# Half chunks of a run-ahead stage spread over the groups beside them, and a residual made in sixteen pieces beside another projection

## The chip, the cores and the metric

One core of a Trainium2 chip runs the whole kernel. The metric is device time in microseconds of one execution; three runs of the kernel before gave 2915.17, 2918.57 and 2919.74 us, median 2918.57 us. TensorE is called PE here, VectorE DVE, ScalarE ACT, GpSimd POOL and SyncE SP.

## What is computed

One decoder layer over 16 meta tokens and 1,024 positions of width 1,024, in float32. The reference, cut to what matters here:

```python
h = layer_norm(concat([meta, x]), ln_emb_g, ln_emb_b)
q, k, v, xr, gr = split(h @ w_in)                      # 5 x 512 columns
attn = stick_breaking(q, k, v)                         # 8 heads
lru = rg_lru(causal_conv(xr)) * gelu(gr)               # gated linear recurrence
mixed = concat([rms_norm(attn), rms_norm(lru)]) @ w_out
h = layer_norm(ALPHA * h + mixed, ln1_g, ln1_b)
# PEER: 8 heads pick 16 of 128 x 128 experts for every token
s1, s2 = q1 @ keys1, q2 @ keys2; idx, g = top_k of the sums, softmax
act = gelu(down[idx] . h); ffn = sum(g * act * up[idx])
h = layer_norm(ALPHA * h + ffn, ln2_g, ln2_b); return h[16:]
```

## The kernel before

The tokens lie in tiles of 128. The program has these stages.

**Front.** Nine tiles `xt` of x are loaded and normalised in place (line 281), transposed and split into a high and a low float32r part `hT`. Each product is three matmuls (`mm3`, lines 127 to 129). While the tiles come, the first two columns of the recurrence's input are projected (`convs`). Then the residual ALPHA * (g * xt + b) is made on DVE from the tiles where they lie (lines 306 and 307, two operations of 128x1024 for each of 8 tiles) and stored by SP to `xh_d` (line 308). The buffers of `xt` are freed with that. Next come the convolution (line 354), the value projection (`values`, in two halves of 256 columns, with its weights split into `v` on ACT and DVE by lines 123 and 124), the gates (line 366, from weights that POOL clears at line 361), the recurrence and the gate branch. Attention follows. In its last quarter `lru_load` reads the residual back (line 561).

**Queries.** Scores and top-16 for six of the eight token tiles. Between them `run_ahead` does chunks of the dense part.

**The dense part.** For the first five tiles (640 tokens) every expert is computed. The experts are 128 chunks of 128. A chunk's down product is two halves of 24 matmuls of 128x320 into the PSUM tile `dps` (`down_gelu`, line 854), each half evicted with a gelu by ACT (line 861). A chunk that is run ahead takes a prepared weight (`take`, line 838: one load in flight, one weight split by ACT and DVE ahead) and its result goes to DRAM, `ge_d`, and comes back later as `gex` (line 1124). 56 chunks are run ahead before: 2 in the output mix, 23 among the queries, 31 in the gate-matrix stage, by the table `RAG = (6, 7, 6, 6, 6)`.

**Gate-matrix stage** (lines 1005 to 1037). For each of five tiles `j` there are 16 groups of 8 tokens. A group compares on DVE (`bt`, `ae`, lines 1020 and 1025), scales on ACT (`at_`, line 1027, eight times), multiplies on PE (`g`, line 1030, 8 products, which the profile shows as 16 matmuls), evicts on ACT into `gst` (line 1031), does one gathered row of a sparse tile on DVE (`hyb`) and a step of the top-16 of the last two tiles (`topk_turn`). Every fourth group SP writes `gst`, 2 MB, to `Gd` (line 1035). After the 16 groups of a tile the written order has that tile's run-ahead chunks:

```python
            for c in range(RAG[j]):
                run_ahead()
```

**Main stage.** For the remaining chunks the down product is made, multiplied with the gate matrix read back from `Gd` as `gl` (line 1117), split into `wh` and `wl`, and multiplied with the `up` rows into `ups` and `keep` (line 1161 on). The sparse rows of the last two tiles (`row`, line 898) are gathered beside it in proportion to PE's work (`tick`).

A scheduler orders each engine's instructions when the program is built: it follows the written order as a priority and its own estimate of times, except where an instruction is pinned. Each engine then runs its list in order, and each DMA queue too.

Of the kernel before, what the change touches and what calls it, by code (L numbers as in the profile page):

```python
# [8 lines left out]
F32 = mybir.dt.float32  # L9
# [5 lines left out]
ALU = mybir.AluOpType  # L15
# [54 lines left out]
RAG = (6, 7, 6, 6, 6)  # L70
RAM = {7: 2}
RA = sum(RAM.values()) + sum(RAQ.values()) + sum(RAG)
# [4 lines left out]
def layer_kernel(ctx, tc, x, meta, vecs, chan, lnc, w_in, gate_w, w_out, wq, skT, down, downT, up, out, dbg=None):  # L77
# [10 lines left out]
    xh_d = dram.tile([S, D], F32, name="xh_d")  # L88
    al_d = dram.tile([KC, P, S], F32, name="al_d")
# [99 lines left out]
    with ExitStack() as c1:  # L189
# [53 lines left out]
        with ExitStack() as c2:  # L243
# [34 lines left out]
            for j0, j1 in LNB:  # L278
                for j in range(j0, j1):
                    n = NM if j == 0 else P  # L280
                    A.activation(xts[j][:n], xts[j][:n], AF.Identity, bias=nm9[:n, j:j + 1], scale=rs9[:n, j:j + 1])
                c0 = 0 if j0 == 0 else NM + (j0 - 1) * P
# [18 lines left out]
            eg = load_vec(ga, 0, "eg")  # L301
            eb = load_vec(ga, 1, "eb")
            A.activation(eg, eg, AF.Copy, scale=ALPHA)
            A.activation(eb, eb, AF.Copy, scale=ALPHA)
            for j in range(1, NT + 1):
                V.tensor_tensor(xts[j], xts[j], eg, op=ALU.mult)
                V.tensor_tensor(xts[j], xts[j], eb, op=ALU.add)
                SY.dma_start(xh_d[(j - 1) * P:j * P, :], xts[j])

        with ExitStack() as c2:  # L310
            vt = ap.tile([P, NB, AW], F32, name="vt")

            with ExitStack() as c3:
# [3 lines left out]
                mps = c3.enter_context(tc.tile_pool(name="mps", bufs=1, space=PSUM, reuse_waits="tile"))  # L317
                sp8 = lr.tile([P, 4], F32, name="sp8")
# [26 lines left out]
                ts_ = [lr.tile([P, T], F32, name=f"t_{i}") for i in range(4)]  # L345

# [32 lines left out]
                def values(half, vh):  # L379
                    for b in range(NB):  # L380
                        t0 = 0 if b == 0 else NM + (b - 1) * P
                        ps = pps.tile([P, 512], F32, name="pp")
                        for c in range(KC):
                            mm3(ps[:, :256], hT[0][:, c, t0:t0 + P], hT[1][:, c, t0:t0 + P], vh[0][:, c], vh[1][:, c], c == 0, c == KC - 1)
                        m = NM if b == 0 else P
                        A.activation(vt[:m, b, half * 256:half * 256 + 256], ps[:m, :256], AF.Copy)

# [15 lines left out]
                for i in range(4):  # L403
                    sq = l2.tile([P, T], F32, name="ig")
                    V.tensor_tensor(sq, rs_[i], rs_[i], op=ALU.mult)
                    V.scalar_tensor_tensor(ts_[i], sq, 1.0, ts_[i], op0=ALU.add, op1=ALU.mult)
                    A.activation(ts_[i], ts_[i], AF.Sqrt)
                    V.tensor_tensor(ys[i], ys[i], ts_[i], op=ALU.mult)
                    V.tensor_tensor_scan(ts_[i], rs_[i], ys[i], 0.0, op0=ALU.mult, op1=ALU.add)
                ms = mps.tile([P, NT], F32, name="ms")  # L410
# [147 lines left out]
            def lru_load(j):  # L558
                mh, ml = mixed(4, j)
                hr = wr.tile([P, D], F32, name="raw")  # L560
                SY.dma_start(hr, xh_d[j * P:(j + 1) * P, :])
# [292 lines left out]
    def down_gelu(c, dps, ge, tick=None):  # L854
        hi, lo = ddn.pop(c)
        for i in range(2):
# [5 lines left out]
            if tick:  # L862
                tick(KC * 3 * HN)

    ra = iter(range(RA))

    def run_ahead():
        c = next(ra)
        ddn[RAS[c]] = take()
        ge = geps[0].tile([P, NF], F32, name="ge")  # L870
        down_gelu(RAS[c], dps1, ge)
        SY.dma_start(ge_d[c], ge)
# [73 lines left out]
    with ExitStack() as c1:  # L946
# [55 lines left out]

        iob = gc.tile([P, NKEYS, AEW], BF16, name="iob")
        G.iota(iob, pattern=[[1, NKEYS], [0, AEW]], base=0, channel_multiplier=0, allow_small_or_imprecise_dtypes=True)
        for j in range(DF):
# [9 lines left out]
            for t0 in range(0, P, GB):  # L1015
                st = gb.tile([P, NKEYS // 2, GB, 2], F32, name="gst")
                for t8 in range(t0, t0 + GB, 8):
# [15 lines left out]
                    topk_turn(DF * P // 8)  # L1033
                blk = (j * P + t0) // GB
                SY.dma_start(Gd[:, :, blk].rearrange("g p f -> p g f"), st.rearrange("p (g a) t b -> p g (a t b)", a=GI // 2))
            for c in range(RAG[j]):
                run_ahead()
# [211 lines left out]
```

## Time and profile before

| | |
|---|---|
| Median of three runs | 2918.57 us |
| The profiled execution | 2921.73 us, its span 2919.9 us |
| Busy in the span: PE, DVE, ACT, POOL | 2771.6, 2468.0, 1146.0, 1224.4 us |
| DMA over the span | 736.32 MB, 252 GB/s |
| Chunks run ahead | 56 of 128 |

The stages show in the stretches of time: the front ends near 75 us, the first matmul of line 1030 starts at 1053.6 us, the last gate group is evicted at 1463.8 us, the first `ups` matmul starts at 1504.07 us, and the last matmuls end near 2903 us. A busy PE is not yet PE at its peak: matmuls are pipelined and their durations overlap, so the distance from start to start is read, not the duration.

### The profile page before, as it was taken

Reading aid. Unit: us, or ns where it says so; the run is one execution under the profiler, and the core shown is the slowest. Engines: PE = TensorE matmul, PEld = TensorE weight load, DVE = VectorE, ACT = ScalarE, POOL = GpSimd, SP = SyncE. Lnnn points to the kernel's source line nnn. Section 1 sums busy time; section 2 is a strip of 40 time slices with the busy share of each in tenths; the row PEclk is TensorE's granted clock in tenths of the full one; section 3 lists DMA queues with packets and bytes.
Section 4 is the critical chain, followed back from the end, with each engine's and each line's share of the span. In section 5 each row is a group of like instructions: output and inputs, shape, how many; then the busy total and the mean of one; then the engine's idle time right before and its main releaser. Section 6 shows DMA issues by size and latency. Waiting matters only on the chain.

```text
span 2919.9 us, 44345 instructions
## 1 busy us (share of the span) xinstructions
PE 2771.6 (95%) x16311; PEld 2490.4 (85%) x16311; DVE 2468.0 (85%) x4768; ACT 1146.0 (39%) x2245; POOL 1224.4 (42%) x1028
## 2 busy tenths in 40 slices
PE   5999999999899987999999999999999999999997
PEld 5998777789899986989988888888888888888886
DVE  8345666769999999689869999999999999999996
ACT  5444554552122268578832222222222232222232
POOL 0002320232333444134325565665555566666653
PEclk9999999999999999899999999999999999999999
DMA  5113134414677778698889999999999999999981
GB/s 176 46 59 88 42 88 151 145 57 148 224 240 230 246 235 276 202 290 252 262 292 351 349 347 353 345 351 361 343 350 355 350 337 358 360 342 369 334 312 73
DMA packets 353946, 736.32 MB, mean 252 GB/s; under 512 B 26032, under 2 KB 164272, under 8 KB 353728
## 3 DMA queue, kind: packets, MB, share of 16 engines
q0 software_dynamic: 113152, 411.16, 39.7%
q1 hardware_dynamic: 235968, 320.23, 32.6%
q8 instruction: 128, 2.10, 0.3%
q10 hardware_dynamic: 4608, 2.10, 0.3%
q14 instruction: 90, 0.74, 0.1%
HBM read 645.24 MB, written 79.69 MB: 248 GB/s over the span
## 4 chain that ended last, share of the span: by engine, by line
PE 50%; DVE 15%; issue 6%; POOL 3%; ACT 3%; DMA 2%; SPq 0%; POOLq 0%; DVEq 0%; ACTq 0%
PE dps L127 6%; PE dps L129 6%; PE dps L128 6%; PE ups L127 6%; PE ups L128 6%; PE ups L129 6%; PE g L1030 5%; DVE row L113 4%; POOL row L898 3%; DVE dl L124 2%; PE keep L129 2%; PE keep L128 2%; PE keep L127 2%; ACT gst L1031 1%; DMA row<-down,idx 1%
## 5 line engine op out<-in xcount | busy, mean ns | idle before, releaser
L127 PE MATMUL dps<-hTd,dl 128*128 128x320 f32 x2048 | 645.2, 315 | 33.8 <-DVE dl L124 26.1
L129 PE MATMUL dps<-hTd,dh 128*128 128x320 f32 x2048 | 641.2, 313 | 0.0
L128 PE MATMUL dps<-hTd,dh 128*128 128x320 f32 x2048 | 641.0, 313 | 0.0
L898 POOL DMA_INDIRECT row<-down,idx x256 | 357.7, 1397 | 226.1 <-DVE act L113 182.0
L898 POOL DMA_INDIRECT row<-up,idx x256 | 343.7, 1342 | 229.2 <-DVE h1s L1086 192.0
L127 PEld LDWEIGHTS dps<-hTd,dl 128*128 128x128 f32 x2048 | 388.9, 190 | 38.4 <-DVE dl L124 20.2
L127 PE MATMUL ups<-uh,wl 128*128 128x512 f32 x1024 | 406.3, 397 | 0.4 <-DVE wl L124 0.4
L128 PE MATMUL ups<-uh,wh 128*128 128x512 f32 x1024 | 406.3, 397 | 0.0
L129 PE MATMUL ups<-ul,wh 128*128 128x512 f32 x1024 | 405.5, 396 | 0.0
L128 PEld LDWEIGHTS dps<-hTd,dh 128*128 128x128 f32 x2048 | 388.9, 190 | 3.0
L129 PEld LDWEIGHTS dps<-hTd,dh 128*128 128x128 f32 x2048 | 388.3, 190 | 0.1
L1086 DVE SCALAR_TENSOR_TENSOR h1s<-row,gws,h1s 128x1024 f32<-128x1024 f32 x256 | 328.3, 1282 | 16.1 <-DMA row<-up,idx 14.0
L113 DVE CUSTOM_DVE_ANT_0 row<-row,h1s 128x1024 f32<-128x1024 f32 x256 | 307.5, 1222 | 33.9 <-DMA row<-down,idx 33.1
L123 ACT ACTIVATE wh<-gl 128x640 fp32r<-128x640 f32 x128 | 101.3, 792 | 575.9 <-DVE gl L1142 315.0
L898 POOL DMA_INDIRECT row<-up,idh x128 | 189.7, 1482 | 305.5 <-DVE acc L1076 95.8
L898 POOL DMA_INDIRECT row<-down,idh x128 | 162.2, 1268 | 245.1 <-DVE ach L113 106.3
L124 DVE TENSOR_TENSOR dl<-raw,dh 128x1024 fp32r<-128x1024 f32 x144 | 179.7, 1248 | 80.5 <-ACT dh L123 80.0
L129 PEld LDWEIGHTS ups<-ul,wh 128*128 128x128 f32 x1024 | 192.8, 188 | 47.3
L127 PEld LDWEIGHTS ups<-uh,wl 128*128 128x128 f32 x1024 | 192.8, 188 | 45.2 <-DVE wl L124 0.8
L128 PEld LDWEIGHTS ups<-uh,wh 128*128 128x128 f32 x1024 | 192.8, 188 | 43.9
L123 ACT ACTIVATE uh<-raw 128x1024 fp32r<-128x1024 f32 x128 | 133.5, 1057 | 191.1 <-PE keep L128 171.2
L1176 DVE TENSOR_TENSOR acc<-acc,ups 128x512 f32<-128x512 f32 x252 | 171.9, 682 | 16.8 <-PE ups L129 16.6
(577 smaller groups left out, 5948.1 us busy)
## 6 DMA issues: line engine op xcount, KB each, us to landing
raw<-downT SPq DMA_DIRECT2D x128, 512.0 KB
raw<-up SPq DMA_DIRECT2D x128, 512.0 KB
Gd<-gst SPq DMA_DIRECT2D x20, 2048.0 KB
gl<-Gd SPq DMA_DIRECT2D x128, 320.0 KB
ge_d<-ge SPq DMA_DIRECT2D x56, 320.0 KB
gex<-ge_d SPq DMA_DIRECT2D x56, 320.0 KB
wraw<-w_in SPq DMA_DIRECT2D x20, 512.0 KB
raw<-wq SPq DMA_DIRECT2D x16, 512.0 KB
```

The lines of the kernel that those rows point to most:

```text
L113: return lambda *a, **k: pin(getattr(V, name)(*a, **k))
L123: A.activation(hi, src, AF.Copy)
L124: V.tensor_tensor(lo, src, hi.bitcast(F32), op=ALU.subtract)
L127: PE.matmul(o, ll, rh, start=start, stop=False, **kw)
L128: PE.matmul(o, lh, rh, start=False, stop=False, **kw)
L129: PE.matmul(o, lh, rl, start=False, stop=stop, **kw)
L898: G.indirect_dma_start(out=row, out_offset=None, in_=src, in_offset=bass.IndirectOffsetOnAxis(ap=ix, axis=0))
L1030: PE.matmul(gpt[:, q], bt[:, q], at[:, q], start=True, stop=True)
L1031: A.activation(st[:, :, t8 - t0:t8 - t0 + 8].rearrange("p a t b -> p t a b"), gpt.rearrange("p t (a b) -> p t a b", b=2), AF.Copy)
L1086: pin(V.scalar_tensor_tensor(h1s[:, j], row, gws[:, j, s:s + 1], h1s[:, j], op0=ALU.mult, op1=ALU.add))
L1176: V.tensor_tensor(h1[j][:, hsl], h1[j][:, hsl], ps, op=ALU.add)
```

## The change

It has two parts. The run-ahead chunks of the gate-matrix stage are no longer written behind each tile's groups: a generator `aheads` gives a chunk in two halves, and after each of the 80 groups `ahead_turn` takes halves until 68 of them are spread evenly (the condition gives 0.85 of a half for each group). With `RAG = 34` instead of 31 there are 59 chunks run ahead and 69 left for the main stage.

The residual is no longer made from the resident tiles: SP stores each normalised tile as it is to `xh_d`, and a generator `residuals` later reads half a tile (128x512) by POOL's queue into one buffer `rt`, does the same two operations on DVE and writes it by POOL's queue to `xr_d`; one step is asked for after each of the value projection's 18 blocks. The scales are loaded and multiplied on ACT as halves, too. `lru_load` reads `xr_d`.

```diff
-RAG = (6, 7, 6, 6, 6)
+RAG = 34
...
                     A.activation(xts[j][:n], xts[j][:n], AF.Identity, bias=nm9[:n, j:j + 1], scale=rs9[:n, j:j + 1])
+                    if j > 0:
+                        SY.dma_start(xh_d[(j - 1) * P:j * P, :], xts[j])
...
-            eg = load_vec(ga, 0, "eg")
-            eb = load_vec(ga, 1, "eb")
-            A.activation(eg, eg, AF.Copy, scale=ALPHA)
-            A.activation(eb, eb, AF.Copy, scale=ALPHA)
-            for j in range(1, NT + 1):
-                V.tensor_tensor(xts[j], xts[j], eg, op=ALU.mult)
-                V.tensor_tensor(xts[j], xts[j], eb, op=ALU.add)
-                SY.dma_start(xh_d[(j - 1) * P:j * P, :], xts[j])
...
+                rx = c3.enter_context(tc.tile_pool(name="rx", bufs=1, reuse_waits="tile"))
...
+                def residuals():
+                    for hf in range(2):
+                        cs = slice(hf * 512, hf * 512 + 512)
+                        gb = []
+                        for i in range(2):
+                            t = rx.tile([P, 512], F32, name=f"rv{i}")
+                            G.dma_start(t, vecs[i, cs].partition_broadcast(P))
+                            A.activation(t, t, AF.Copy, scale=ALPHA)
+                            gb.append(t)
+                        for j in range(NT):
+                            t = rx.tile([P, 512], F32, name="rt")
+                            G.dma_start(t, xh_d[j * P:(j + 1) * P, cs])
+                            V.tensor_tensor(t, t, gb[0], op=ALU.mult)
+                            V.tensor_tensor(t, t, gb[1], op=ALU.add)
+                            G.dma_start(xr_d[j * P:(j + 1) * P, cs], t)
+                            yield
+                res = residuals()
...
                         A.activation(vt[:m, b, half * 256:half * 256 + 256], ps[:m, :256], AF.Copy)
+                        next(res, None)
...
-                SY.dma_start(hr, xh_d[j * P:(j + 1) * P, :])
+                SY.dma_start(hr, xr_d[j * P:(j + 1) * P, :])
...
     def down_gelu(c, dps, ge, tick=None):
+        for _ in down_halves(c, dps, ge, tick):
+            pass
+
+    def down_halves(c, dps, ge, tick=None):
...
+            yield
...
+    def aheads(n):
+        for _ in range(n):
+            c = next(ra)
+            ddn[RAS[c]] = take()
+            ge = geps[0].tile([P, NF], F32, name="ge")
+            for i, _ in enumerate(down_halves(RAS[c], dps1, ge)):
+                if i == 1:
+                    SY.dma_start(ge_d[c], ge)
+                yield
...
+        ahead = aheads(RAG)
+        gone = [0]
+        def ahead_turn(groups):
+            while gone[0] * groups < turn[0] * 2 * RAG:
+                next(ahead, None)
+                gone[0] += 1
...
                     topk_turn(DF * P // 8)
+                    ahead_turn(DF * P // 8)
...
-            for c in range(RAG[j]):
-                run_ahead()
+        next(ahead, None)
```

In PE's listing the half-chunk matmuls stand so. Ahead of the first matmul of line 1030: 1,370 before and 1,370 now. Between the first and the last of line 1030: 1,174 before, in three blocks of 288, 192 and 144 and some interleaved stretches, with 32 of the 80 groups that have none ahead of the next; now 1,462, exactly 24 behind 36 of the groups, and none behind 7. From the last of line 1030 to the first `ups`: 240 before, 100 now. After it: 3,360 before, 3,212 now. Between the front's gates and the first gate group PE's list is the same.

DVE in the front, before: the tail of the third block's splits (`hT`), the residual (`xt`), the convolution (`y`) and the weights of the values (`v`).

```order
L306 TENSOR_TENSOR xt<-xt,eg 128x1024 x2
L307 TENSOR_TENSOR xt<-xt,eb 128x1024 x2
L306 TENSOR_TENSOR xt<-xt,eg 128x1024 x2
L307 TENSOR_TENSOR xt<-xt,eb 128x1024 x2
L352 TENSOR_SCALAR y_631<-xr,ch 128x1040
L333 MEMSET t_630 128x4
L352 TENSOR_SCALAR y_632<-xr,ch 128x1040
L354 SCALAR_TENSOR_TENSOR y_631<-xr,ch,y_631 128x1040
L329 TENSOR_SCALAR t_628<-t_627 128x4
L124 TENSOR_TENSOR v_678<-wraw,v_677 128x8x128
```

And now the same place, where the pieces (`rt`, lines 354 and 355 of the changed kernel) stand among the splits:

```order
L354 TENSOR_TENSOR rt<-rt,rv_724 128x512
L301 TENSOR_TENSOR hT_89<-tm,hT_88 128x384 x3
L298 CAST hT_88<-tm 128x384
L355 TENSOR_TENSOR rt<-rt,rv_727 128x512
L301 TENSOR_TENSOR hT_89<-tm,hT_88 128x384
L328 MEMSET t_612 128x4
L125 TENSOR_TENSOR v_660<-wraw,v_659 128x8x128
L366 TENSOR_SCALAR y_613<-xr,ch 128x1040
L324 TENSOR_SCALAR t_610<-t_609 128x4
L368 SCALAR_TENSOR_TENSOR y_613<-xr,ch,y_613 128x1040
L325 RECIPROCAL t_610<-t_610 128x4
L125 TENSOR_TENSOR v_660<-wraw,v_659 128x8x128
```

The eight residual operations ahead of `v` are gone, the first `v` stands ahead of the convolution, and four of the sixteen pieces stand ahead of it in all.

POOL's queue, now, where before only the clearing of `gw` stood (the pieces' loads and stores):

```order
L353 DMA rt<-xh_d 128x512
L241 MEMSET xr 128x3
L375 MEMSET gw_1209 128x128
L356 DMA xr_d<-rt 128x512
L375 MEMSET gw_1222 128x128
L353 DMA rt<-xh_d 128x512
L241 MEMSET xr 128x3
L356 DMA xr_d<-rt 128x512
```

The loads and stores of the single buffer alternate, and the clearing for later gates stands between them.

ACT in the gate-matrix stage, before, among groups without half chunks:

```order
L1031 ACTIVATE gst<-g 128x8x64x2
L1027 ACTIVATE at__11643<-ae,sT 128x128 x8
L1031 ACTIVATE gst<-g 128x8x64x2
L1027 ACTIVATE at__11698<-ae,sT 128x128 x8
L1031 ACTIVATE gst<-g 128x8x64x2
L1027 ACTIVATE at__11726<-ae,sT 128x128 x8
```

And now, in the second half of the stage (`ge` is the gelu of a half chunk, `dh` the split of the next weight):

```order
L1064 ACTIVATE at__13581<-ae,sT 128x128 x8
L882 ACTIVATE ge<-dps 128x320
L1068 ACTIVATE gst<-g 128x8x64x2
L1064 ACTIVATE at__13646<-ae,sT 128x128 x8
L882 ACTIVATE ge<-dps 128x320
L124 ACTIVATE dh<-raw 128x1024
L1068 ACTIVATE gst<-g 128x8x64x2
L1064 ACTIVATE at__13701<-ae,sT 128x128 x8
```

Before, a `gst` evicts the group whose `at_` stand just ahead of it. Now it evicts the group before that one: `at__13646` is made ahead of the eviction of the group of `at__13581`.

## Rows read from the trace of the kernel before

**Rows 1.** Stretches: us; busy us of PE, PEld, DVE, ACT, POOL; PEclk; DMA share; GB/s.

```profile
54.50:75.00 20.50, 6.95 (x22) 5.25 (x21) 20.29 (x26) 7.73 (x11) 0.10 (x1) 0.60 0.48 176
...
1053.60:1464.00 410.40, 368.93 (x2528) 355.17 (x2528) 355.68 (x952) 325.62 (x816) 148.48 (x104) 0.96 0.82 257
1464.00:1504.00 40.00, 37.02 (x240) 36.75 (x239) 15.29 (x15) 13.85 (x20) 3.78 (x4) 0.95 0.87 298
1504.00:2899.00 1395.00, 1390.63 (x7185) 1214.18 (x7184) 1294.93 (x1612) 367.08 (x484) 809.66 (x590) 1.00 0.92 336
...
1073.60:1098.70 25.10, 25.07 (x186) 24.33 (x187) 25.10 (x72) 24.37 (x62) 14.11 (x9) 1.00 1.04 333
```

**Rows 2.** Waits of DVE, 1504 to 2899 us: us in total, times, longest.

```profile
DVE row L113 <- DMA row<-down,idx: 33.1, 43, 2.4
```

**Rows 3.** Stretches, tile dps alone (half chunks): busy us of PE, PEld, ACT.

```profile
1073.60:1098.70 25.10, 17.78 (x83) 13.02 (x83) 1.26 (x3) 1.00 1.04 333
1053.60:1464.00 410.40, 215.89 (x1176) 179.17 (x1177) 21.50 (x50) 0.96 0.82 257
1464.00:1504.00 40.00, 37.02 (x240) 36.72 (x238) 3.88 (x9) 0.95 0.87 298
1504.00:2899.00 1395.00, 504.85 (x3362) 499.45 (x3360) 60.71 (x141) 1.00 0.92 336
```

**Rows 4.** PE timeline (start us, us, ...), half-chunk matmuls one behind the other.

```profile
1500.70 0.31 PE L128 MATMUL dps<-hTd,dh 128*128 128x320 f32 x1
...
1503.92 0.31 PE L129 MATMUL dps<-hTd,dh 128*128 128x320 f32 x1
```

**Rows 5.** Gate-matrix stage, PE timeline, groups without half chunks; [idle before <-releaser].

```profile
1128.56 2.58 PE L1030 MATMUL g<-at__11726,bt 128*128 128x128 f32 x16 [1.43 <-ACT at__11726 L1027]
1132.57 2.59 PE L1030 MATMUL g<-at__11770,bt 128*128 128x128 f32 x16 [1.43 <-ACT at__11770 L1027]
```

**Rows 6.** Gate-matrix stage, ACT timeline, the same groups.

```profile
1128.11 2.48 ACT L1027 ACTIVATE at__11726<-ae,sT 128x128 f32<-128x128 bf16 x8
1131.18 1.05 ACT L1031 ACTIVATE gst<-g 128x1024 f32<-128x1024 f32 x1 [0.58 <-PE g L1030]
```

**Rows 7.** SP's queue after the last gate group.

```profile
1464.91 0.37 SPq L1035 DMA_DIRECT2D Gd<-gst  x1
```

**Rows 8.** Front, PE timeline.

```profile
54.00 0.62 PE L129 MATMUL pp<-hT,wh 128*128 128x384 f32 x2
58.90 0.58 PE L127 MATMUL pp<-v,hT 128*128 128x256 f32 x1 [4.29 <-ACT v L123]
...
69.39 0.58 PE L129 MATMUL pp<-v,hT 128*128 128x256 f32 x1 [9.26 <-DVE v L124]
```

**Rows 9.** Front, DVE timeline.

```profile
60.67 2.35 DVE L307 TENSOR_TENSOR xt<-xt,eb 128x1024 f32<-128x1024 f32 x2
...
68.14 1.19 DVE L124 TENSOR_TENSOR v<-wraw,v 128x1024 fp32r<-128x1024 f32 x1
```

**Rows 10.** Front, ACT timeline.

```profile
54.48 0.87 ACT L241 ACTIVATE xr<-pp 128x384 f32<-128x384 f32 x2 [3.48 <-PE pp L129]
...
56.40 1.28 ACT L328 ACT_TABLE_LOAD   x1
...
57.81 1.04 ACT L123 ACTIVATE v<-wraw 128x1024 fp32r<-128x1024 f32 x1
```

**Rows 11.** POOL timeline: DMAs from POOL's queue and the copy behind them.

```profile
239.34 0.51 POOL L543 DMA_DIRECT2D QS<-qh  x1 [9.15 <-ACT qh L538]
239.94 0.51 POOL L544 DMA_DIRECT2D QS<-ql  x1
...
242.90 0.52 POOL L471 CAST qz<-QS 64x128 fp32r<-64x128 f32 x2 [1.44 <-DMA QS<-qh]
```

**Rows 12.** DVE timeline after the second half of the value projection.

```profile
161.96 1.24 DVE L369 TENSOR_TENSOR y<-y,ig 128x1040 f32<-128x1040 f32 x1 [23.71 <-ACT ig L367]
```

**Rows 13.** Line 534, POOL's DMA issues: ns min/median/max, first and last start.

```profile
L534 POOL DMA_DIRECT2D KS<-kh x16: 509/529/744, 227.9 to 391.6; - x16
```

More of the change, by code (lines that the diff above doesn't have):

```diff
@@ L69 @@
 RAQ = {i: 1 + (i > 7) for i in range(1, 16)}
-RAG = (6, 7, 6, 6, 6)
+RAG = 34
 RAM = {7: 2}
-RA = sum(RAM.values()) + sum(RAQ.values()) + sum(RAG)
+RA = sum(RAM.values()) + sum(RAQ.values()) + RAG
 RAS = sorted([1 + 4 * i for i in range(min(RA, 32))] + [2 + 4 * i for i in range(RA - 32)])
@@ L88, in layer_kernel @@
     xh_d = dram.tile([S, D], F32, name="xh_d")
+    xr_d = dram.tile([S, D], F32, name="xr_d")
     al_d = dram.tile([KC, P, S], F32, name="al_d")
@@ L409, in layer_kernel @@
                     V.tensor_tensor_scan(ts_[i], rs_[i], ys[i], 0.0, op0=ALU.mult, op1=ALU.add)
+                for _ in res:
+                    pass
                 ms = mps.tile([P, NT], F32, name="ms")
@@ L854, in down_gelu @@
     def down_gelu(c, dps, ge, tick=None):
+        for _ in down_halves(c, dps, ge, tick):
+            pass
+    def down_halves(c, dps, ge, tick=None):
         hi, lo = ddn.pop(c)
@@ L863, in down_gelu @@
                 tick(KC * 3 * HN)
+            yield
     ra = iter(range(RA))
-    def run_ahead():
[L868 to L872, printed above, removed]
+    def aheads(n):
[7 more added lines that the diff above has]
+                yield
+    def run_ahead():
+        for _ in aheads(1):
+            pass
     mpx.close()
```

## The prediction

> **What bounds the kernel now.** The profiled execution took 2921.73 us, 3.2 us more than the median of the runs (2918.57); the sum is made against the profiled time, and 3.2 us come off at the end. A measurement of this kernel can tell some 0.2%, 5.8 us, from no change.
>
> I read the stretches of time first, since the share of busy time mixes stages [rows 1]. Two stages matter, and they differ. In the main stage PE is busy for 1390.63 of 1395.00 us: it is bound by PE, with DVE (1294.93 us) and DMA (0.92) not far behind. In the gate-matrix stage with its tail up to the first `ups` (410.40 + 40.00 = 450.4 us) no engine is full: in the 410.40 us PE has 368.93, DVE 355.68, ACT 325.62, DMA 0.82. So it is the order that bounds it, and it has two textures. From 1073.6 to 1098.7 us gate groups and half chunks alternate, and PE, DVE and ACT are busy for 25.07, 25.10 and 24.37 of 25.10 us [rows 1]. In the main stage DVE waits for gathered rows for 33.1 us [rows 2]; it has little slack there either. The mixed stretch holds 83 matmuls of half chunks [rows 3] and six groups.
>
> One half-chunk matmul takes (1503.92 − 1500.70) / 22 = 0.146 us, start to start (the two rows have 21 others between them) [rows 4]; a half of 24 takes 3.51 us, a chunk 7.03. So in the mixed stretch 83 × 0.146 = 12.15 us went to half chunks and 12.95 us to six groups with the few small products beside them: **2.16 us a group**. Where groups stand alone they come every 132.57 − 128.56 = **4.01 us**, with PE idle for 1.43 of them [rows 5]: ACT makes eight `at_` (2.48 us), waits 0.58 us for PE's tail and evicts for 1.05 us [rows 6], and PE waits for the next `at_`. ACT and PE take turns, and nothing fills PE's turn.
>
> What the stage would need on PE alone: 80 × 2.16 = 173 us, and 1,174 + 240 = 1,414 matmuls of half chunks at 0.146 us, 207 us: 380 us. It takes 450.4, so 70 us are lost there.
>
> **Part one, the half chunks.** The order now puts a half behind most groups, 1,462 + 100 = 1,562 matmuls in the same stage, a need of 173 + 229 = 402 us. Whether the filling works depends on ACT's order, and the listing answers it: `at_` of a group now stands ahead of the eviction of the group before it, so a half on PE (3.51 us) covers the next `at_`. A group then needs on PE 2.16 + 0.85 × 3.51 = 5.1 us. On ACT it needs 2.48 + 1.05 us and 0.85 eviction of a half, 21.50 / 50 = 0.43 us each [rows 3], about 3.9 us, with the split of a weight 4.4; on DVE 355.68 / 80 = 4.4 us and the splits of a few more weights [rows 1]. PE is the longest of the three, by 0.5 us. I take 402 us, plus some 5 us for the end of the stage: behind the last group the list holds only 100 matmuls (14.7 us), while the last 2 MB of `Gd` have to be written, which begins about 1 us after the last eviction [rows 7], read back, multiplied and split. At the 298 GB/s of that stretch [rows 1] the writing alone is 7 us; with the read and the first multiplications I estimate 18 to 20 us. And 5 us more, since DVE and DMA will be nearly full and small waits add up. 412 us against 450.4: **−38 us**. The ends: were six groups of the mixed stretch to take only the span of `g`'s own matmuls, somewhat under 2.16, and no wait be left, −56; were every hole to come back in another place, 0.
>
> The weights of the half chunks go through the same single load and split as before; three more chunks are three more loads of 0.5 MB, and their write to `ge_d` and read back as `gex` goes beside them at a DMA share of 0.82: nothing on the path, and if DMA had no room, the load of 0.52 MB and the write of 0.33 MB of a chunk at 257 GB/s, 10 us for three [rows 1].
>
> **Part two, chunks moved out of the main stage.** Its list loses 3,360 − 3,212 = 148 matmuls, which are 148 × 0.146 = **−21.7 us** if PE stays the bound. That they cost nothing where they go is in the 402 us above. DVE's work does not fall with them but for the splits of three weights: 1,295 of then 1,373 us, 94%. The ends are −21.7 and 0. The start of the main stage can be less well supplied than before, since 240 matmuls stood ahead of it and 100 stand there now: **+3 us**, between 0 and the 140 × 0.146 = 20 us of cover that go.
>
> **Part three, the residual.** After the last convolution matmul at 54.0 us PE waits for `v` on ACT for 4.29 us and then for `v` on DVE for 9.26 us, until 69.39 us [rows 8]: DVE does the residual's operations, 2.35 us for two, and reaches `v` at 68.14 us [rows 9]. Now the first `v` of DVE stands ahead of the convolution and of 12 of the 16 pieces. What stays: ACT evicts `xr`, loads a table for 1.28 us and makes the first `v` by 58.85 us [rows 10]; and DVE's 1.19 us follow, so that the products that wait for DVE start at about 60 us in place of 69.4. I take **−9 us**; the ends are −13.5 (both waits gone) and 0 (`v` held by its weights' load).
>
> The pieces then cost nothing if they come in time and nobody stands behind them. A piece is an issue by POOL, a load, two operations of DVE on 128x512 and an issue for the store, and with one buffer the next load waits for that store. By the nearest rows: issue 0.51 us, from the second issue's end (240.45) to the copy that waits for it (242.90) 2.4 us of landing [rows 11], two operations of half of 1.18 us, and another issue and landing: 7 us in all, 16 of them 112 us, and a reload of the scales in the middle. Starting at some 24 us, they end near 150 us. DVE's next use behind the value projection is at 161.96 us, after 23.71 us of idleness [rows 12], and by the term above moves to some 152 us. So the cover holds, with few microseconds to spare. POOL clears `gw` between the pieces, and those clearings wait behind a store that waits for DVE; the gates that need them come late in the projection. The sixteen loads and stores are 8 MB more over the front's DMA, which has a share of 0.48 [rows 1]: nothing. If the last piece is late, DVE's list waits with it.
>
> What speaks against this part is who issues the DMAs. POOL's issues beside a busy DVE take 509 to 744 ns, median 529 [rows 13], so DVE holds them up by 0.2 us at most there. In the Trainium skill, the page "SBUF — State Buffer", section "SBUF: two separate sides", warns that a DMA from GpSimd's queue can starve for descriptors while VectorE holds the shared port pair, and advises ACT's or SP's queue instead. [...]
>
> **Sum:** −9 − 38 − 21.7 + 3 = −66 us; 2921.7 − 66 = 2856 us for a profiled execution, **2853 us** for the median.
>
> **The rivals.**
>
> *Spread without gain.* The halves fill holes of PE, but DVE or DMA turn up as the next bound of the stage: DVE has 355.68 us of work in it, DMA was at 1.04 of its share in the mixed stretch [rows 1], and each half now waits for a weight that is split by an ACT and a DVE that serve groups as well. Then the stage stays near 445 us, and only the moved chunks and the front are left: −9 − 21.7 − 5 + 3 = −33, 2886 us. For it speaks that all three engines are full in the mixed stretch; against it that this stretch had six groups in 25.1 us with 14 matmuls for each, 4.2 us of DVE a group, while the whole stage would now give DVE longer for a group (19.5 matmuls a group, 5.0 us on PE).
>
> *Pieces late.* If every piece waits for one more DVE operation of 1.2 us at its load and its store, its period is 9.4 us and the sixteen end at 177 us: the gates' DVE work at 152 us starts 25 us late, of which about 5 are slack. +20, 2882 us for the rest as forecast. [...] The issue rows [rows 13] speak against it.
>
> *Slower.* The half stands inside the turn of ACT and PE. If ACT evicts a group ahead of the next `at_`, as it does now for lone groups, and PE's list has the half between group and group, a group takes 4.01 + 3.51 + 0.43 = 7.9 us. About 61 groups with a half and 19 without give 561 us, in place of 450: +111 − 21.7 + 3 − 9, some 3005 us. It decides from a mean period of 5.7 us on, where 80 groups take the 450 us of before, plus what the other terms give back, 6.0. Against it stands ACT's listing, one group ahead, in the second half.
>
> *Main stage not bound by PE.* If DVE or the gathered rows set its pace, the 148 matmuls less give nothing: 2875 us. The 33.1 us of waits for rows [rows 2] speak for it, PE's 1390.63 of 1395 us against it.
>
> **Chances.** Forecast 0.72 (its own range 2833 to 2878), spread without gain 0.15, pieces late 0.06, main stage not bound by PE 0.04, slower 0.03. The range goes from 2833 (stage at its need, −56) to 2890, which takes in the three rivals that are still faster. Faster by over 0.2%: 0.94; within 0.2%: 0.03, the part of "spread without gain" where another 25 us go wrong too; slower: 0.03.
>
> **What would show it.** The stretch from the first gate matmul to the first `ups` is 405 to 420 us long, with PE busy above 0.95 in it and waits of PE for `at_` gone behind most groups; it is wrong if the stretch stays above 435. From the first `ups` to the last matmul there are 1370 to 1378 us with PE still full; it is wrong if DVE or DMA ends most waits there. Near 55 to 60 us PE waits some 5 us once, for ACT, and the 9.26 us behind DVE are gone. Pieces come every 7 us, and the DVE operation of 161.96 us starts at 150 to 154 us; at 160 or later the front's gain is lost. A mean period of the groups above 5.7 us would make the whole forecast wrong.

## The result and the profile after

The changed kernel takes 2869.34 us (median of four runs, 2864.7 to 2871.8) against 2916.87 us before (four runs); ratio 0.9836, interval 0.9817 to 0.9855, so about 47.5 us faster. The forecast said 2853, with 2833 to 2890 as its range. The profiled execution is the fastest of the four (span 2862.8), that of before slower than any of its four (span 2919.9), so between the two traces 57.1 us have to be accounted for:

| us | before | now | difference | forecast |
|---|---|---|---|---|
| start to first gate matmul | 1053.7 | 1049.9 | −3.8 | −9 |
| first gate matmul to first `ups` | 450.4 | 397.9 | −52.5 | −38 |
| first `ups` to the end of the last matmul | 1399.1 | 1396.1 | −3.0 | −18.7 |
| behind the last matmul | 16.7 | 18.9 | +2.2 | 0 |

The sum was nearly met by terms that were not. One trace of each kernel is compared here, and stages differ between traces of the same lists of instructions: in nine traces with the residual as before (this one and those of experiments below) the first gate matmul starts between 1047.5 and 1053.7 us, and in four other traces that have the chunks in blocks as before the stretch from it to the first `ups` takes 444.6 to 448.0 us, not 450.4. So the −3.8 is within the scatter, and some 2 to 6 of the −52.5 us are this one trace of before. The main stage of before, then the two stages of the changed kernel, columns as in [rows 1]:

```profile
1504.07:2903.20 1399.13, 1394.76 (x7202) 1217.19 (x7200) 1298.99 (x1622) 368.11 (x486) 811.71 (x591) 1.00 0.92 335
```

```profile
1049.90:1447.70 397.80, 390.33 (x2914) 384.36 (x2913) 372.68 (x970) 341.78 (x842) 145.91 (x108) 1.00 0.92 292
1447.70:2843.90 1396.20, 1381.78 (x7053) 1199.05 (x7052) 1295.11 (x1622) 356.25 (x478) 822.10 (x591) 0.99 0.93 338
```

In the gate-matrix stage PE is now busy for 390.33 of 397.80 us. In the main stage it has 148 matmuls fewer than before and is busy for 13 us less, but the stage is only 3 us shorter: 14.4 us without work now, 4.4 before. ACT's timeline in the second half of the gate-matrix stage, with its PE counterpart:

```profile
1244.74 2.51 ACT L1064 ACTIVATE at__13581<-ae,sT 128x128 f32<-128x128 bf16 x8
1247.23 0.44 ACT L882 ACTIVATE ge<-dps 128x320 f32<-128x320 f32 x1
1249.01 1.12 ACT L1068 ACTIVATE gst<-g 128x1024 f32<-128x1024 f32 x1 [1.35 <-PE g L1067]
1250.01 2.49 ACT L1064 ACTIVATE at__13646<-ae,sT 128x128 f32<-128x128 bf16 x8
```

```profile
1247.03 1.95 PE L1067 MATMUL g<-at__13512,bt 128*128 128x128 f32 x16
...
1252.33 1.95 PE L1067 MATMUL g<-at__13581,bt 128*128 128x128 f32 x16
```

A group comes every 5.30 us with a whole half chunk behind it (so in 36 of the 80; the mean over all is 4.78), against 4.01 us without one before [rows 5]. Eight `at_` of the next group (1244.74) are done before PE reaches it (1252.33), and PE's lines carry no idle time in brackets; in [rows 5] each had 1.43 us. A group costs PE 5.30 − 3.51 = 1.79 us beside the half.

In the front (DVE, then PE, then ACT, in order of time):

```profile
39.02 0.69 DVE L354 TENSOR_TENSOR rt<-rt,rv 128x512 f32<-128x512 f32 x1 [5.23 <-DMA rt<-xh_d]
39.63 0.55 DVE L301 TENSOR_TENSOR hT<-tm,hT 128x384 fp32r<-128x384 f32 x1
...
162.96 0.69 DVE L354 TENSOR_TENSOR rt<-rt,rv 128x512 f32<-128x512 f32 x1 [7.51 <-DMA rt<-xh_d]
163.68 0.69 DVE L355 TENSOR_TENSOR rt<-rt,rv 128x512 f32<-128x512 f32 x1
164.29 1.24 DVE L420 TENSOR_TENSOR ig<-r 128x1040 f32<-128x1040 f32 x1
165.56 1.24 DVE L421 SCALAR_TENSOR_TENSOR t<-ig,t 128x1040 f32<-128x1040 f32 x1
166.72 1.24 DVE L383 TENSOR_TENSOR y<-y,ig 128x1040 f32<-128x1040 f32 x1
```

```profile
64.06 0.39 PE L128 MATMUL pp<-v,hT 128*128 128x256 f32 x1 [1.53 <-ACT v L124]
...
65.32 0.38 PE L130 MATMUL pp<-v,hT 128*128 128x256 f32 x1 [0.52 <-DVE v L125]
...
169.67 0.69 PE L128 MATMUL pp<-hT,wl 128*128 128x384 f32 x1 [5.59 <-ACT gg L437]
```

```profile
40.27 0.67 ACT L295 ACTIVATE tm<-tr,lc 128x384 f32<-128x384 f32 x1 [4.01 <-DVE hT L301]
...
166.84 1.07 ACT L422 ACTIVATE t<-t 128x1040 f32<-128x1040 f32 x1 [4.98 <-DVE t L421]
```

PE's waits of 4.29 and 9.26 us [rows 8] are down to 1.53 and 0.52 us. But the products of the values start at 64.06 us, not at 58.90: the third block of x is late. On DVE's list the split of 39.63 us stands behind a piece that waited 5.23 us for its load, and ACT waited 4.01 us for that split. At the other end the last piece waits 7.51 us for its load, and with it the recurrence's operations behind it; ACT waits 4.98 us for those and PE 5.59 us for ACT's gelu, where it had waited 1.59 us before (at 169.53 us, below). The operation of 161.96 us [rows 12] starts at 166.72. The first query product starts at 247.2 us, 2.9 us later than before (244.3).

```profile
169.53 0.44 PE L127 MATMUL pp<-hT,wl 128*128 128x384 f32 x1 [1.59 <-ACT gg L420]
```

Waits in the main stage (us in total, times, longest): two of DVE before, that [rows 2] does not have, then DVE's and PE's now:

```profile
DVE h1s L1086 <- DMA row<-up,idx: 14.0, 27, 1.3
DVE acc L1076 <- DMA row<-up,idh: 3.8, 8, 1.1
```

```profile
DVE row L114 <- DMA row<-down,idx: 39.0, 50, 2.6
DVE h1s L1123 <- DMA row<-up,idx: 21.2, 27, 3.0
DVE wl L125 <- ACT wh L124: 13.9, 17, 0.9
DVE acc L1213 <- PE ups L130: 9.2, 6, 2.1
DVE ul L125 <- ACT uh L124: 7.7, 4, 3.4
DVE acc L1113 <- DMA row<-up,idh: 3.0, 6, 1.1
```

```profile
PE dps L128 <- ACT gex L882: 7.5, 4, 5.7
PE ups L128 <- DVE acc L1213: 4.4, 7, 1.2
PE ups L128 <- DVE wl L125: 2.3, 1, 2.3
```

DVE waits 39.0 us for `down` rows, where it was 33.1 [rows 2], and 21.2 for `up` rows (14.0 before); with the third kind (`idh`) that is 63.2 us in place of 50.9. PE in turn waits for DVE (`acc`, `wl`) and for gelus of ACT. The longest of these waits stands near the end, where the layer norm of a finished sparse tile comes between (ACT, then PE):

```profile
2793.14 0.20 ACT L147 ACTIVATE lnrs<-lnve 128x1 f32<-128x1 f32 x1 [3.13 <-DVE lnve L162]
...
2797.29 1.28 ACT L882 ACT_TABLE_LOAD   x1
2798.58 0.77 ACT L882 ACTIVATE gex<-dps 128x320 f32<-128x320 f32 x2
```

```profile
2799.07 0.64 PE L128 MATMUL dps<-hTd,dl 128*128 128x320 f32 x1 [5.74 <-ACT gex L882]
```

ACT waits for DVE's `lnve`, and a table load stands ahead of the gelu. After PE's 5.74 us without work the granted clock is 0.50 from 2799.1 to 2804.3 us (1.2 in place of 2.4 GHz), and matmuls of half chunks start 0.267 us apart there in place of 0.146.

To compare main stages I count **lost time**: what the starts of the matmuls lie further apart than where nothing disturbs them, 0.146 us for 128x320 [rows 4] and 0.234 us for 128x512; waits are in it, and the matmuls at the lower clock behind a long one. Before it is 6.4 us, now 25.2 us, of which some 8 lie in the last 70 us of the stage, around the wait just shown.

### The profile page after: what moved, and what is told of

It is laid out like the page before. It is cut to its first block, busy times and chain, and to the rows that moved or that the text cites. A ratio compares the mean times of both kernels' runs of the same rounds, so it can differ in the third digit from the quotient of the medians.

```text
span 2862.8 us, 44485 instructions
## 1 busy us (share of the span) xinstructions
PE 2741.0 (96%) x16311; PEld 2464.7 (86%) x16311; DVE 2467.1 (86%) x4784; ACT 1137.5 (40%) x2247; POOL 1247.5 (44%) x1064
## 4 chain that ended last, share of the span: by engine, by line
PE 31%; DVE 20%; issue 11%; DMA 8%; POOL 7%; ACT 2%; POOLq 0%; DVEq 0%; SPq 0%; ACTq 0%
POOL row L927 7%; DMA row<-up,idx 6%; DVE row L114 5%; PE g L1067 4%; PE dps L128 4%; PE dps L129 4%; PE dps L130 4%; PE ups L128 3%; PE ups L129 3%; PE ups L130 3%; DVE dl L125 2%; DVE h1s L1123 2%; DMA row<-down,idx 1%; PE keep L130 1%; DVE ii L718 1%
## 5 line engine op out<-in xcount | busy, mean ns | idle before, releaser
L927 POOL DMA_INDIRECT row<-up,idx x256 | 352.8, 1378 | 218.0 <-DVE h1s L1123 181.1
L1123 DVE SCALAR_TENSOR_TENSOR h1s<-row,gws,h1s 128x1024 f32<-128x1024 f32 x256 | 328.2, 1282 | 23.2 <-DMA row<-up,idx 21.2
L130 PEld LDWEIGHTS ups<-ul,wh 128*128 128x128 f32 x1024 | 193.8, 189 | 47.5
L124 ACT ACTIVATE dh<-raw 128x1024 fp32r<-128x1024 f32 x144 | 151.7, 1053 | 47.9 <-DMA raw<-downT 47.9
```

The costliest lines, as they stand in the source:

```text
L124: A.activation(hi, src, AF.Copy)
L130: PE.matmul(o, lh, rl, start=False, stop=stop, **kw)
L927: G.indirect_dma_start(out=row, out_offset=None, in_=src, in_offset=bass.IndirectOffsetOnAxis(ap=ix, axis=0))
L1123: pin(V.scalar_tensor_tensor(h1s[:, j], row, gws[:, j, s:s + 1], h1s[:, j], op0=ALU.mult, op1=ALU.add))
```

## The experiments

**Theories.** *Main stage held by DVE:* as soon as chunks leave it, DVE's list, which runs in order and has the arrival of 583 gathered rows in it (256, 256 and 71), sets the pace, and PE's lost time eats what the chunks gave. Rival: PE is the bound, and the holes are chance. *Residual:* its pieces bring nothing. Rival: the −3.8 us at the first gate matmul are theirs. Ratios are to the kernel before, run beside each group of experiments.

**e1, the spread alone, and e2, the pieces alone.** e1 is the changed kernel with the residual as before; e2 is the kernel before with the new residual.

```diff
 # e2, on the changed kernel
-RAG = 34
+RAG = (6, 7, 6, 6, 6)
...
-                    ahead_turn(DF * P // 8)
...
+            for c in range(RAG[j]):
+                run_ahead()
```

> The spread of the half chunks with 34 chunks, the residual made as before. Theory (the residual's pieces bring nothing: in the changed kernel the first query DMA stands at 242.3 us, 3 us later than before, although value products start 4 us earlier): as fast as the changed kernel or up to 8 us faster, 2861 to 2870 us. Rival (the forecast's -9, or the 3.7 us by which the first gate group came earlier, is the pieces' work): 4 to 9 us slower than the changed kernel, 2873 to 2878 us.

> The residual in sixteen pieces alone, the chunks in blocks of 6, 7, 6, 6 and 6 as before. Theory: no gain, 2913 to 2922 us against 2917 of before; DVE waits for rt loads ahead of the splits of the third block of x, the last piece ends near 164 us, and PE waits some 5 us for ACT's gelu at 165 to 170 us. Rival (forecast): -9, 2908 us.

e1: 2863.57 us, 0.9822 (0.9809 to 0.9835), as the theory had it. The first query product starts at 242.3 us, 4.9 us earlier than with the pieces; the first gate matmul at 1049.3, so that the −3.8 us there do not come from the pieces; they are no more than the scatter of that start. e2: 2929.60 us, 1.0052 (1.0039 to 1.0065), 15 us slower: worse than the theory said. In its profile the front costs 3.4 us up to the first query product, which are gone again by the first gate matmul (1053.6 us, as before); the gate-matrix stage is 5.8 us shorter and the main stage 9.9 us longer than before, though from the gate branch on every engine's list is the same as before:

```profile
1498.20:2907.20 1409.00, 1397.90 (x7202) 1218.78 (x7200) 1299.53 (x1623) 362.79 (x486) 815.13 (x591) 1.00 0.91 333
```

**e3, 34 chunks in blocks, and e4, 31 chunks spread,** both with the residual as before: with before and e1 a table of two by two.

```diff
 # e3, on the kernel before
-RAG = (6, 7, 6, 6, 6)
+RAG = (7, 7, 7, 7, 6)
 # e4, on e1
-RAG = 34
+RAG = 31
```

> 34 chunks in the gate-matrix stage, but in blocks of 7, 7, 7, 7 and 6 behind the tiles, the residual as before. Theory (the main stage is held by DVE once chunks leave it: of the 21.7 us that PE needs less there only 3 arrive): the gate-matrix stage gets 21 us longer, the main stage 3 to 8 us shorter, in all 2930 to 2935 us. Rival (chunks moved at no price for DVE): the main stage gets 21 us shorter, 2917 us in all.

> The spread with 31 chunks, as many as before, the residual as before. Theory (gate-matrix stage bound by PE, main stage by DVE as soon as chunks leave it): the gate-matrix stage is some 20 us shorter than with 34 spread chunks, 378 us, the main stage only 3 us longer, 1399 us, so that the whole is 2843 to 2852 us. Rival 1 (the main stage bound by PE): what one stage gives the other takes, the same time as with 34, 2861 to 2870 us. Rival 2 (DVE, 365 us busy of 379 there, holds the gate-matrix stage too): only 8 us shorter, 2855 to 2862 us.

```profile
1051.80:1511.60 459.80, 418.57 (x2911) 405.07 (x2910) 372.49 (x968) 343.40 (x842) 151.85 (x107) 0.98 0.80 261
1511.60:2899.40 1387.80, 1377.45 (x7058) 1197.28 (x7056) 1292.48 (x1620) 356.73 (x477) 809.48 (x591) 1.00 0.92 337
```

```profile
1051.40:1422.50 371.10, 365.26 (x2674) 353.91 (x2673) 359.04 (x954) 331.28 (x825) 147.08 (x104) 0.99 0.91 291
...
1441.50:2841.50 1400.00, 1397.04 (x7197) 1219.19 (x7196) 1299.79 (x1624) 369.29 (x487) 813.80 (x591) 1.00 0.92 338
```

| profiled stages, us | gate-matrix stage | main stage | lost time in main | ratio |
|---|---|---|---|---|
| before (31, blocks) | 450.4 | 1399.1 | 6.4 | 1 |
| e3 (34, blocks) | 459.8 | 1387.8 | 16.3 | 1.0036 (1.0024 to 1.0048) |
| e4 (31, spread) | 390.1 | 1400.0 | 7.9 | 0.9814 (0.9801 to 0.9827) |
| e1 (34, spread) | 398.1 | 1399.4 | 28.5 | 0.9822 (0.9809 to 0.9835) |

Spreading is worth 60 us of the stage at either number of chunks (54 to 58 at 31 against the four other traces with blocks) and is the whole gain. Three chunks more bring nothing over all; in blocks they cost 0.36%. In the main stage 144 matmuls of e4, worth 21.1 us, brought 0.6 us to e1, and the lost time grew by 20.6: the theory's point. In the gate-matrix stage e4 is 8.0 us shorter than e1, not 20, and the total fell into rival 2's range, by which DVE holds this stage too. One reckoning gives the 8 us without that rival: a group lasts 5.30 us with a half and 4.01 us without one, so that a half adds 1.29 us and not its own 3.51; six halves fewer are 7.7 us. But e4's trace has hardly any lone groups (4 of 80 have no half-chunk matmul behind them), and DVE is busy there for 359.04 of 371.10 us, 4.49 us a group, more than PE's own steps take (16 of 0.112 us and on average 16.5 of 0.146, some 4.2 us). So rival 2 is not excluded; what holds e4's stage was not tried by itself and stays open. In e3 the main stage did give 11.3 us, more than the theory's 3 to 8, but in one of the fastest of its ten runs (2918.0 us; they lie between 2916.4 and 2930.6). Its median of 2926.25 us against 2914.41 lies between theory and rival.

**e5 and e6, where e2's main stage lost its time.** e5 writes each piece back where it was read; e6 is the kernel before with the residual in the second array.

```diff
 # e5, on e2
-    xr_d = dram.tile([S, D], F32, name="xr_d")
-                            G.dma_start(xr_d[j * P:(j + 1) * P, cs], t)
+                            G.dma_start(xh_d[j * P:(j + 1) * P, cs], t)
-                SY.dma_start(hr, xr_d[j * P:(j + 1) * P, :])
+                SY.dma_start(hr, xh_d[j * P:(j + 1) * P, :])
 # e6, on the kernel before
+    xr_d = dram.tile([S, D], F32, name="xr_d")
-                SY.dma_start(xh_d[(j - 1) * P:j * P, :], xts[j])
+                SY.dma_start(xr_d[(j - 1) * P:j * P, :], xts[j])
-                SY.dma_start(hr, xh_d[j * P:(j + 1) * P, :])
+                SY.dma_start(hr, xr_d[j * P:(j + 1) * P, :])
```

> The residual's pieces alone as in e2, but each piece is written back to xh_d where it was read, so that the array xr_d is not there and all later arrays in DRAM lie where they lay before. e2 was 15 us slower than before with the same order of instructions on every engine from the gate branch on; its main stage was 10 us longer. Theory A (where the arrays lie in DRAM makes the gathered rows later): 2911 to 2919 us, about as before, the main stage back at 1399 us. Theory B (the pieces themselves, by the time at which everything behind them runs): 2926 to 2931 us, as e2.

> The kernel before, only that the residual is written to and read from a second array xr_d of 4 MB, declared behind xh_d, which stays unused: the order is the same, the later arrays lie 4 MB further. Theory A (place in DRAM): 2924 to 2931 us. Theory B (the pieces): as before, 2914 us within 4 us.

e5: 2921.70 us, 1.0018 (1.0009 to 1.0027). e6: 2917.76 us, 1.0004 (0.9994 to 1.0014). e5 is free of some two thirds of e2's 15 us, as theory A says, but e6, which has the array and not the pieces, is as before, against it. Neither theory stands. In the four profiles of this one order the main stage lasts 1399.1 (before), 1402.5 (e5), 1405.0 (e6) and 1409.0 us (e2), with lost times of 6.4, 9.7, 12.2 and 16.4 us: it swings by 10 us. DVE's waits for rows in them are 50.9, 55.1, 54.4 and 71.2 us, so that the arrival of rows goes with e2's long stage but does not order the others. What made e2 slow in all five of its runs stays open.

**e7, half of one sum on DVE left out, and e8, the rows spread a little longer.**

```diff
 # e7, on e1
-                    pin(V.scalar_tensor_tensor(h1s[:, j], row, gws[:, j, s:s + 1], h1s[:, j], op0=ALU.mult, op1=ALU.add))
+                    pin(V.scalar_tensor_tensor(h1s[:, j, :512], row[:, :512], gws[:, j, s:s + 1], h1s[:, j, :512], op0=ALU.mult, op1=ALU.add))
 # e8, on e1
-SPF = 0.95
+SPF = 0.98
```

> As e1 with 34 spread chunks, but the multiply-add of the gathered up rows to h1s, 256 of them, is done on the first 512 of 1,024 columns only, so that half of that sum is left out: 150 to 165 us less work for DVE in the main stage, the gathers and all of PE's work as in e1. Theory (DVE's list holds PE in the main stage, 28.5 us more than PE's own steps in e1): the main stage falls from 1399 to 1370 to 1378 us, in all 2835 to 2842 us. Rival (the rows' transfers hold it, however little DVE has to do): at most 8 us less, above 2855 us.

> As e1, but the gathered rows are spread over 98% of PE's work in the main stage in place of 95%, so that DVE has 3% less to do in each microsecond until they are through. Theory (DVE's list is the bound): main stage 5 to 12 us shorter, 2851 to 2859 us against 2864 of e1. Rival 1 (bound by PE with holes by chance): the same within 4 us. Rival 2 (the end is bound by the last rows and the layer norms behind them): 10 us or more slower.

Main stages of e1 and e7, and e7's longest waits of DVE in it; then the main stage and the end of e8:

```profile
1447.40:2846.80 1399.40, 1382.37 (x7053) 1199.16 (x7052) 1294.74 (x1622) 356.80 (x478) 811.58 (x591) 0.99 0.92 337
1447.20:2819.00 1371.80, 1371.80 (x7053) 1194.64 (x7052) 1170.02 (x1620) 362.92 (x478) 765.53 (x591) 1.00 0.93 344
```

```profile
DVE h1s L1106 <- DMA row<-up,idx: 92.2, 97, 2.4
DVE row L113 <- DMA row<-down,idx: 37.7, 52, 2.1
```

```profile
1448.30:2824.90 1376.60, 1373.37 (x7053) 1194.95 (x7052) 1289.32 (x1609) 362.16 (x474) 806.79 (x590) 1.00 0.94 343
2824.90:2845.10 20.20, 0.00 (x0) 0.00 (x0) 15.19 (x34) 5.43 (x7) 10.21 (x5) 0.56 0.32 130
```

e7: 2838.28 us, 0.9736 (0.9722 to 0.9751). PE's list is the same in e1, e7 and e8; DVE's is ordered anew in e7 from about 1926 us on, and in e8 in the whole stage. With 125 us less on DVE (150 to 165 were expected) and the same gathers PE is busy in every microsecond of the main stage, 1371.8 us, lost time 0.8: the 27.6 us that e1's stage takes more were lost to DVE's work. The rows do not hold it: DVE, with more time, now waits 92.2 us for `up` rows (24.9 in e1), and PE loses nothing by that. e8: 2845.49 us, 0.9757 (0.9743 to 0.9770), 18 us faster than e1, more than the 5 to 12 expected; lost time 5.5 us. The room for that stood at the end of the stage: in the last twentieth DVE was busy for 52.92 of 69.80 us in the changed kernel, and is for 64.99 of 68.80 in e8. It leaves nothing out: **e8 beats both kernels**.

**e9 to e12, the same rate of rows with the other parts.** e9 is the whole change with 0.98; e10 has DVE's part of the pieces pinned to the written order in addition (`W` does that); e11 is the kernel before with 0.98; e12 is e1 with 1.0.

```diff
 # e9, on the changed kernel; e11, on the kernel before
-SPF = 0.95
+SPF = 0.98
 # e10, on e9
-                            V.tensor_tensor(t, t, gb[0], op=ALU.mult)
-                            V.tensor_tensor(t, t, gb[1], op=ALU.add)
+                            W.tensor_tensor(t, t, gb[0], op=ALU.mult)
+                            W.tensor_tensor(t, t, gb[1], op=ALU.add)
 # e12, on e1
-SPF = 0.95
+SPF = 1.0
```

> The whole change, with the gathered rows over 98% of PE's work as in e8, so that the main stage no longer hides or adds anything by DVE; against e8 (0.9757 of before, 2845.5 us) it tells what the residual's pieces are worth. Theory (they cost the 3 to 5 us by which the first query product comes later, 247 against 242 us): 2845 to 2851 us. Rival 1 (the forecast's -9): 2836 us. Rival 2 (they lengthen the main stage, as e2 showed with 15 us): 2855 us or more.

> As e9, with DVE's two operations of each piece kept in the written order, so that on DVE's list no piece stands among the splits of the third block and all 16 stand behind the first gates, the last ones among the recurrence's operations. Theory (two harms in the front, waits for rt among the splits and the last pieces ahead of the recurrence): the first value product comes at 56 to 58 us in place of 64.1, but PE still waits 5 us or more for ACT's gelu at 160 to 175 us, and the first query product comes at 243 to 249 us; in all within 4 us of e9. Rival (the early pieces are the only harm): the first query product at 238 us or before, 5 to 9 us less than e9.

> The kernel before with the rows over 98% of PE's work. Theory (DVE holds the main stage only once chunks leave it; before, PE's steps lacked only 6 us): 0 to 6 us less than before, 2911 to 2917 us. Rival (the rows' rate costs every version the same): 15 to 18 us less, 2899 to 2902 us.

> As e8, with the rows over all of PE's work. Theory (main stage of e8 1376.6 us against PE's own need of some 1371: what is left of DVE's hold is 5 us, and rows that end with the matmuls make the end longer): 2841 to 2852 us. Rival (DVE is still the bound at 98%): 8 us or more less, under 2838 us.

e9: 2851.93 us, 0.9771 (0.9758 to 0.9784). Against e8 the pieces cost 0.14%, 4 us; the intervals overlap a little, so that the cost itself is not certain, but the rival's −9 us is excluded. In the two profiles the first query product is 3.7 us later and the span 4.4 us longer, the main stages alike (1377.3 and 1376.6 us).

e10: 2850.38 us, 0.9770 (0.9754 to 0.9785), the same as e9. PE's timeline:

```profile
56.39 0.39 PE L128 MATMUL pp<-v,hT 128*128 128x256 f32 x1 [0.43 <-ACT v L124]
...
58.08 0.38 PE L130 MATMUL pp<-v,hT 128*128 128x256 f32 x1 [0.81 <-DVE v L125]
...
127.74 2.52 PE L380 MATMUL gp<-y,gw 128*128 128x272 f32 x4 [3.71 <-issue]
...
164.28 0.44 PE L128 MATMUL pp<-hT,wl 128*128 128x384 f32 x1 [0.63 <-ACT gg L437]
```

With no piece among the splits, the values start at 56.39 us, 6.9 us earlier than in e9 (63.33): the first harm is shown. The second was misjudged: PE waits 0.63 us for the gelu, not 5 or more, since the recurrence's operations stand ahead of the last pieces now. What it waits for is 3.71 us ahead of a gate product. The trace names no releaser, but DVE's list shows a likely one:

```profile
125.62 0.69 DVE L114 TENSOR_TENSOR rt<-rt,rv 128x512 f32<-128x512 f32 x1 [1.50 <-DMA rt<-xh_d]
126.23 1.29 DVE L368 SCALAR_TENSOR_TENSOR y<-xr,ch,y 128x1040 f32<-128x1040 f32 x1
```

The last operation of a convolution ends at 127.52 us, 0.22 us ahead of that product, and stands behind a piece that waited for its load. The first query product comes at 240.8 us, between theory (243 to 249) and rival (238), and the total shows nothing of the 5.2 us against e9; e10's runs lie between 2846.2 and 2856.2 us, so that this much can't be read from them.

e11: 2916.41 us, 0.9986 (0.9977 to 0.9995), 4 us faster: with PE as the bound the rows' rate is worth what little was lost, as the theory had it.

e12: 2863.03 us, 0.9811 (0.9798 to 0.9825), some 16 us slower than e8 by the ratios, more than the theory's range, with its cause:

```profile
1446.20:2818.30 1372.10, 1372.10 (x7053) 1194.86 (x7052) 1278.21 (x1573) 362.95 (x465) 814.72 (x583) 1.00 0.94 342
2818.30:2857.50 39.20, 0.01 (x1) 0.00 (x0) 32.48 (x71) 10.83 (x17) 24.58 (x11) 0.53 0.30 118
```

The main stage is at PE's own need, 1372.1 us, 4.5 us better than in e8, but behind the last matmul stand 39.2 us, 19.0 us more than e8's 20.2: the last rows end with the matmuls, and the layer norms of their tiles come behind.

## Why the prediction was right, and where it was not

**Part one** was right in its mechanism and too cautious in size. Groups come one ahead on ACT, and a half fills PE's turn. Measured −52.5 for −38, within the end of −56. That 397.9 us lie so near the 402 worked out from the mixed stretch is in part luck: a group costs PE 1.79 us in place of 2.16, 30 us less over 80 groups. By its own steps PE needs 80 × 1.79 = 143 us, 1,562 × 0.146 = 229 us and 8 us for the 72 small matmuls among the 2,914, 380 us in all, and the stage took 18 us more. Some 4 of these lie in the end behind the last group (1429.3 to 1447.8, 18.5 us, as estimated), which was filled but for 3.2 us; the others lie among the groups, where DVE is nearly as full as PE (372.68 and 390.33 of 397.80 us). The 10 us added for the end and for small waits came on top of a 2.16 that covered them already.

**Part two failed**, at the step "−21.7 us if PE stays the bound", with DVE at "94%" taken as room. DVE's 1,295 us are what it does, not what it needs: its list also waits, 63 us for rows alone (39.0 + 21.2 + 3.0), and it does not go on to other work meanwhile. 1,295 and 63 are 1,358 of the 1,371 us that PE needs by its own steps, 99%; before they were 1,299 and 51 of 1,393, 97%. Over the traces this share goes with the lost time, though not strictly: 95.0% and 0.8 us in e7; 96.9% and 6.4 us before, 97.1% and 7.9 in e4; 98.4% and 5.5 in e8, 98.5% and 16.3 in e3; 99.1% and 25.2 now, 99.4% and 28.5 in e1. (DVE's waits for ACT and PE don't belong in it: with them the list comes near the whole stage in every trace, before too.) This was the rival "main stage not bound by PE", with a chance of 0.04; the 2869 us measured lie nearer to its 2875 than to the 2853 of the forecast. [rows 2] beside [rows 1] pointed at it: 1,295 + 33 of 1,373 us is 97%, and the `up` rows, which [rows 2] leaves out, make it 98%. The cause itself is shown by e7, and e8 agrees. The +3 for the start was right in kind: the first dozen `ups` matmuls lost 2.3 us, at 0.42 us each in place of 0.234, where before they lost 0.7.

**Part three failed** in its sign: +4 by e9 against e8, if only by ratios whose intervals overlap; the first query product comes at 244.7 to 247.7 us in the four traces with the pieces in this order and at 242.2 to 244.3 in the nine without them, 3.6 us later on average. The −3.8 us at the first gate matmul were not its work, since e1 has them without it. "The products that wait for DVE start at about 60 us" held the last convolution product where it was; it moved from 54 to beyond 62 us, and they start at 65.32, because pieces stand among the splits that lead to it, which the order listing of the change shows, and each waits for its load. I had counted what the pieces take on DVE, not what DVE waits for in them. "7 us in all" for a piece was 9.0 us (143.6 us from the first load's issue at 21.1 to the last store's at 164.7, by 16). The transfers were not the reason as a rule: counted from the start of the issue, a load lands in 3.1 us and a store in 2.3 (medians), together no more than the 5.8 that the forecast had for both. What came on top are hand-overs, DVE's other work between a landing and the store, and single late landings (loads up to 5.8 us). So the rival "pieces late" came true in its place, the recurrence, but not by its cause. POOL's issues took 538 to 557 ns, all 32 of them; the trap that the Trainium skill describes on "SBUF — State Buffer", in "SBUF: two separate sides", does not show in them. The slowest load, 5.8 us from 33.13 us on, is no sign of it either, since DVE stood idle for the 5.23 us ahead of using it (39.02, above); the DMA engines moved 304 GB/s meanwhile, at a share of 0.86. A third harm was not seen at all: the first transpose comes at 15.97 us in place of 13.56. In the five kernels traced that load `rv` at 1.6 us beside x it comes at 15.9 to 16.0, in the nine others at 12.9 to 13.6; that `rv` is the reason wasn't tried separately.

So −66 was −57 between the traces and −47.5 between medians: 14 us better in one term, 16 and 5 worse in two others, 2 at the end. That the total lies in the range owes to these opposite errors.

## What to carry to other kernels

An alternation of two engines that wait for each other is filled by giving one of them half-sized independent work in each turn; that was worth some 50 us here, and the spread, not the number of pieces, made it. Before moving work off the bounding engine, add the runner-up's waits for arriving data to its busy time, since an engine that runs its list in order can't use them: here an engine busy for 1,295 of 1,373 us had with them 98 to 99%, and of 21.7 us only 3 arrived. Look also where its room lies: the average hid an end of the stage at 76%, and rows spread over 98% in place of 95% of PE's work were worth 18 us. A small operation that waits for a transfer costs what stands behind it on its engine; look at its neighbours on the list before calling it covered.

## What was not expected of the hardware

The same lists of instructions from the gate branch on gave main stages of 1399.1, 1402.5, 1405.0 and 1409.0 us, with DVE busy for 1,299 to 1,300 us in each; part of the difference goes with when gathered rows arrive (14.0 us of waits for `up` rows before, 26.5 in e2). So a gain under 10 us in this stage is not read from one trace. That a residual made 1,300 us earlier in another way goes with 15 us more, in all five runs, is measured and not explained.
